# Where the first weight sum of a seven-product matrix multiply is begun: at the fetch of its first block, or at the cast of that block

## The chip, the cores and the metric

The kernel runs on one core of a Trainium2 chip. The metric is device time in microseconds (us) of one execution. Engines are named as in the profile: PE is TensorE (matrix multiplies), ACT is ScalarE, DVE is VectorE, POOL is GpSimd, SP is SyncE. SP issues plain loads; POOL issues the transfers that add into their destination.

## The reference

The program is a small encoder: two layers, 528 tokens (512 and 16 learned ones), width 1024. Each layer has a feed-forward half, a mixer (gated linear attention beside softmax attention) and a second feed-forward half:

```python
def swiglu(x, w_gate, w_up, w_down):
    return (jax.nn.silu(x @ w_gate) * (x @ w_up)) @ w_down
...
for l in range(DEPTH):
    h = h + 0.5 * swiglu(rmsnorm(h, norm_gains[l, 0]), ...)
    h = h + mixer(rmsnorm(h, norm_gains[l, 1]), ...)
    h = h + 0.5 * swiglu(rmsnorm(h, norm_gains[l, 2]), ...)
```

The change concerns the four feed-forward blocks alone. Their hidden width is 2816. In the names of tiles and in this document they are blocks 00, 01, 10 and 11 (layer, then first or second half), in this order of time.

## The kernel before

**Seven products.** A gate and an up column block of 256 hidden channels make one *pair*; there are eleven, numbered 0 to 10. A pair's weights are cut into four blocks called 11, 12, 21 and 22, each a tile of 128 x 1024 float32 (512 KB). Instead of eight products of quarter blocks the kernel makes seven, in the manner of Winograd. Three use a weight block as it was loaded: product 1 uses 11, product 2 uses 12, product 4 uses 22. Four use sums of blocks:

- product 7 uses s3 = 21 - 11,
- product 6 uses s2 = 22 + s3,
- product 5 uses s1 = 21 + 22,
- product 3 uses s4 = s2 - 12.

The first eight pairs' down projections are made the same way; their weights are the entries 11 to 14 (two for each of the first two groups of four pairs). So a feed-forward block has 15 entries in the order 0, 1, 2, 3, 11, 12, 4, 5, 6, 7, 13, 14, 8, 9, 10.

**How a sum is made.** s3 starts as a negation of block 11 on ACT (`negative`, line 203), and POOL then issues a transfer that adds block 21 from DRAM to it (`add`, line 208). s2 starts as a load of block 22 on SP, and POOL adds s3 to it from SBUF. s1 starts as a load of 21, and POOL adds 22 from DRAM. s4 is, from entry 2 on, a subtraction on DVE (line 233); for the entries 0 and 1 it is a negation and an addition as s3 is. In the trace s3 and s4 are the tiles `s`, and s2 and s1 are tiles `w`, so the three additions read `s<-win`, `w<-s` and `w<-win`. s3 and s4 share three buffers (`wsa`), s2 and s1 three others (`wsb`), and loaded blocks three (`wraw`).

**Cast and use.** `make` splits each operand for PE: ACT rounds it to `whi` (line 264), DVE subtracts to get `wlo` (line 265). There are four buffers of each, so a cast can run at most three products ahead of PE: it waits until the product four before it is done. `fetch` runs further ahead, nine loads (`AHEAD_FETCHED`). In steady state the products of two neighbouring pairs alternate in the order 1, 7 (of the pair before), 2, 4 and 3 (of the pair before), 6, 5. Behind products 1, 6 and 7 ACT takes a copy of the PSUM accumulator (line 575, "the copy" below), and the next casts are placed behind that copy. At the end of the first two groups the seven products of the down projection stand between the pairs (line 685, with additions into `h` at line 693 and the casts of their operands at lines 646 and 647). That stretch is called the *group end* below.

**Order.** Each engine works off its instructions strictly in the order in which they stand. That order is not written by hand: a planner goes through the program with priorities in the order of the source and costs of its own, and places an instruction early if it takes its inputs to be ready by then. So an edit in one place can move instructions elsewhere.

Of the kernel before, what the change touches and what calls it, by code (L numbers as in the profile page):

```python
# [14 lines left out]
ALU = mybir.AluOpType  # L15
# [31 lines left out]
OPENING = ((0, 0), 0), ((0, 0), 1)  # L47
# [123 lines left out]
class Weights:  # L171
# [34 lines left out]
    def add(self, t, src):  # L206

        self.nc.gpsimd.dma_start(t, src, accum_op=ALU.add)  # L208

    def sums(self, f, i, product, w):  # L210


        got = self.summed
        if product == "1":
            s3 = self.negative(f, i, "s3", w)
            self.add(s3, self.dram(f, i, "21"))
            s2 = self.block(f, i, "22", self.short, "wsb")
            self.add(s2, s3)
            got[f, i, "7"], got[f, i, "6"] = s3, s2
        if product == "12"[(f, i) in OPENING]:  # L220
            s1 = self.block(f, i, "21", self.short, "wsb")
            self.add(s1, self.dram(f, i, "22"))
            got[f, i, "5"] = s1
        late = 2 <= i
        if product == "2" and not late:
            s4 = self.negative(f, i, "s4", w)
            self.add(s4, got[f, i, "6"])
            got[f, i, "3"] = s4
        if product == "2" and late:
            self.kept = w  # L230
        if product == "6" and late:
            s4 = self.long.tile([P, SLAB], F32, tag="wsa", name=f"s4_{f[0]}{f[1]}_{i}")
            self.nc.vector.tensor_tensor(s4, w, self.kept, ALU.subtract)
            got[f, i, "3"] = s4

    def fetch(self, upto):

        while self.fetched < min(upto, len(self.loads)):
            load = self.loads[self.fetched]
            if isinstance(load, int):  # L240
                w = self.raw.tile([P, SLAB], F32, tag="raw", name=f"raw{load}")
                self.nc.sync.dma_start(w, self.wts[load])
                self.raws[self.fetched] = w
            elif load[2] in DIRECT:
                self.raws[self.fetched] = self.block(*load[:2], DIRECT[load[2]])
                if load[2] == "1" and load[:2] not in OPENING:
                    self.sums(*load, self.raws[self.fetched])
            self.fetched += 1

    def make(self, upto):  # L250
        nc = self.nc
        while self.made < min(upto, len(self.loads)):
            self.fetch(self.made + 1)
            s = self.made
            load = self.loads[s]
            w = self.raws.pop(s, None)
            if w is None:
                w = self.summed.pop(load)
            hi = self.hi_pool.tile([P, SLAB], F32R, tag="whi", name=f"whi{s}")
            lo = self.lo_pool.tile([P, SLAB], F32R, tag="wlo", name=f"wlo{s}")  # L260
            for a in np.split(np.arange(SLAB), 2 if s == 0 else 1):
                cs = slice(a[0], a[-1] + 1)
                with self.tc.issue_after(self.behind) if self.behind else nullcontext():
                    nc.scalar.copy(hi[:, cs], w[:, cs])  # L264
                nc.vector.tensor_tensor(lo[:, cs], w[:, cs], hi[:, cs].bitcast(F32), ALU.subtract)  # L265
            self.got[s] = (hi, lo)
            self.got.pop(s - 12, None)
            self.made += 1
            if not isinstance(load, int) and (load[2] in "26" or load[2] == "1" and load[:2] in OPENING):
                self.sums(*load, w)  # L270

    def use(self, j, ahead=AHEAD_MADE):
# [29 lines left out]
def build(tc, ctx, xt, wts, win, par, w2, const, umask, out):  # L302
# [243 lines left out]
    def ffn(l, f, norm, done, following):  # L546

        x, rs, up, n = norm.x, None, None, live[0]
        w = n // 2
        pools = open_pools("left", psum=("s2",), c=4, s2=2)  # L550
        made, hid, sums, raw, sets = {}, {}, {}, {}, {}
        risen = iter(range(KC))

# [636 lines left out]
    def finish_chunk(c):  # L1190
        fin.square(c)
        gain(c, slice(0, SEQ))

    def ending(sums, operand, rs):

        table("abs_reciprocal_sqrt_and_small")
# [146 lines left out]
```

## Time and profile before

| | |
|---|---|
| time before, median of 3 runs | 2238.69 us (2238.67 to 2239.18) |
| profiled execution: its own time | 2233.24 us |
| profiled execution: its span, first to last instruction | 2231.4 us |
| granted TensorE clock, mean | 0.996 |
| PE busy | 2170.3 us, 97% |
| DVE busy | 1700.7 us, 76% |
| ACT busy | 1244.2 us, 56% |
| POOL busy | 164.4 us, 7% |

The page gives each engine's busy time. The list of waits says which engine sat idle before which instruction, and what ended the wait. The timeline lists instructions of an engine in order of time, with the idle time before each in brackets and its releaser. A table by windows gives busy time, the granted clock of TensorE ("PEclk", 1.00 is full speed) and the share of time in which the 16 DMA engines worked.

### The profile page before, as it was taken

How to read it: one execution, taken by the hardware profiler on the slowest of the kernel's cores; microseconds unless marked ns; L12 is line 12 of the kernel's file. 1: busy time of each engine (PE TensorE's matmuls, PEld its weight loads, DVE VectorE, ACT ScalarE, POOL GpSimd, SP SyncE). 2: the span in 40 equal slices, each digit the busy share in tenths (PEclk: the TensorE clock that was granted, in tenths of full speed). 3: DMA queues.
4: the chain of work that ended last, by engine and by line, in shares of the span. 5: the costliest groups of instructions: out<-in, count | busy, mean ns of one | idle time of the engine just before them, and what ended most of it. 6: DMA issues, size and time to landing. Idle time of an engine off the chain costs nothing. (4 is left out here: it accounts for less than half of the span.)

```text
span 2231.4 us, 40120 instructions
## 1 busy us (share of the span) xinstructions
PE 2170.3 (97%) x16506; PEld 2075.3 (93%) x16506; DVE 1700.7 (76%) x2623; ACT 1244.2 (56%) x1815; POOL 164.4 (7%) x192
## 2 busy tenths in 40 slices
PE   7999999999999999999999999999999999999898
PEld 7999999989999999999999999999788888999897
DVE  8877877577876679687788778676779768687777
ACT  8555555345784555454675455553557836545553
POOL 1111100000000011111011111000000001111100
PEclk9999999999999999999999999999999999999999
DMA  9877753212114577777668777421111237677761
GB/s 280 226 190 203 198 150 109 77 48 72 43 39 133 133 189 191 211 203 190 179 166 212 190 208 202 139 100 67 57 67 57 88 104 199 177 200 191 187 180 67
DMA packets 92647, 330.29 MB, mean 148 GB/s; under 512 B 10288, under 2 KB 12720, under 8 KB 92464
## 3 DMA queue, kind: packets, MB, share of 16 engines
q1 hardware_dynamic: 63440, 226.65, 28.2%
q0 software_dynamic: 27072, 98.58, 24.4%
q8 instruction: 130, 2.13, 0.4%
q10 hardware_dynamic: 1952, 2.50, 0.4%
q14 instruction: 53, 0.43, 0.1%
HBM read 289.94 MB, written 2.10 MB: 131 GB/s over the span
## 5 line engine op out<-in xcount | busy, mean ns | idle before, releaser
L571 PE MATMUL ss<-xc,whi 128*128 128x264 f32 (+1 forms) x4928 | 909.2, 286 | 26.1 <-ACT c L575 16.5
L571 PEld LDWEIGHTS ss<-xc,whi 128*128 128x128 f32 x4928 | 768.8, 190 | 31.1 <-ACT c L575 18.8
L571 PE MATMUL ss<-xc,wlo 128*128 128x264 f32 (+1 forms) x2464 | 702.8, 285 | 2.7 <-DVE wlo L265 2.7
L265 DVE TENSOR_TENSOR wlo<-w,whi 128x1024 fp32r<-128x1024 f32 (+1 forms) x301 | 365.3, 1216 | 152.8 <-ACT whi L264 152.7
L571 PEld LDWEIGHTS ss<-xc,wlo 128*128 128x128 f32 x2464 | 467.4, 190 | 4.3 <-DVE wlo L265 4.3
L264 ACT CAST whi<-w 128x1024 fp32r<-128x1024 f32 (+1 forms) x301 | 312.1, 1048 | 136.2 <-PE ss L571 52.2
L438 PE MATMUL mm<-x,whi 128*128 128x264 f32 (+1 forms) x1712 | 384.8, 315 | 0.0
L438 PEld LDWEIGHTS mm<-x,whi 128*128 128x128 f32 x1712 | 278.4, 188 | 16.6 <-issue 1.0
L438 PE MATMUL mm<-x,wlo 128*128 128x264 f32 (+1 forms) x856 | 266.1, 315 | 0.0
L685 PE MATMUL ss<-g,whi 128*128 128x264 f32 (+1 forms) x1280 | 239.5, 285 | 4.4 <-DVE h L693 3.1
L264 ACT CAST whi<-raw 128x1024 fp32r<-128x1024 f32 x126 | 132.0, 1048 | 163.6 <-PE mm L438 102.8
L685 PEld LDWEIGHTS ss<-g,whi 128*128 128x128 f32 x1280 | 198.6, 188 | 7.0 <-ACT whi L264 3.4
L265 DVE TENSOR_TENSOR wlo<-raw,whi 128x1024 fp32r<-128x1024 f32 x126 | 153.9, 1221 | 59.3 <-ACT whi L264 58.4
L685 PE MATMUL ss<-g,wlo 128*128 128x264 f32 (+1 forms) x640 | 181.2, 283 | 0.0
L575 ACT COPY c<-ss 128x528 f32<-128x528 f32 (+1 forms) x132 | 78.3, 593 | 181.6 <-PE ss L571 181.4
L265 DVE TENSOR_TENSOR wlo<-s,whi 128x1024 fp32r<-128x1024 f32 x120 | 146.5, 1221 | 37.5 <-ACT whi L264 37.5
L438 PEld LDWEIGHTS mm<-x,wlo 128*128 128x128 f32 x856 | 159.6, 188 | 8.5 <-issue 0.7
L438 PE MATMUL ss<-g,whi 128*128 128x264 f32 (+2 forms) x900 | 166.2, 299 | 0.0
L438 PEld LDWEIGHTS ss<-g,whi 128*128 128x128 f32 x900 | 131.7, 188 | 5.3
L264 ACT CAST whi<-s 128x1024 fp32r<-128x1024 f32 x120 | 126.1, 1051 | 10.9 <-PE ss L571 7.2
L208 POOL DMA_DIRECT2D w<-win x60 | 54.5, 908 | 1029.3 <-DVE wlo L265 410.3
L203 ACT ACTIVATE s<-w 128x1024 f32<-128x1024 f32 x68 | 71.6, 1056 | 89.7 <-DMA w<-win 77.9
(265 smaller groups left out, 3405.4 us busy)
## 6 DMA issues: line engine op xcount, KB each, us to landing
w<-win SPq DMA_DIRECT2D x299, 512.0 KB, 5.4
raw<-wts SPq DMA_DIRECT2D x126, 512.0 KB, 3.2
s<-win POOLq DMA_DIRECT2D x60, 512.0 KB, 5.2
w<-s POOLq DMA_DIRECT2D x60, 512.0 KB, 5.5
w<-win POOLq DMA_DIRECT2D x60, 512.0 KB, 7.5
s<-w POOLq DMA_DIRECT2D x8, 512.0 KB, 8.4
h<-xt SPq DMA_DIRECT2D x3, 528.0 KB, 6.3
out<-h ACTq DMA_DIRECT2D x4, 256.0 KB, 2.4
```

Source lines behind the costliest of these rows:

```text
L203: self.nc.scalar.activation(t, w, AF.Copy, scale=-1.0)
L208: self.nc.gpsimd.dma_start(t, src, accum_op=ALU.add)
L264: nc.scalar.copy(hi[:, cs], w[:, cs])
L265: nc.vector.tensor_tensor(lo[:, cs], w[:, cs], hi[:, cs].bitcast(F32), ALU.subtract)
L438: TE.matmul(acc.half[i][:width], lhs, rhs[:, acc.spans[i]], start=first, stop=last)
L571: TE.matmul(acc[:, j], a[:, j, k], b[:, at], start=bool(begin and k == 0 and i == 0), stop=k == len(x) - 1 and i == 2, skip_group_check=no ...
L575: W.behind = S.copy(part(st, q), acc).ins
L685: TE.matmul(acc[:, j], a[:, j, k], xs[b][:, k], start=bool(begin and k == 0 and i == 0), stop=k == 3 and i == 2, skip_group_check=not begin)
```

## The change

For entries from 2 on, the negation for s3 and the two additions behind it (21 into s3, s3 into s2) are no longer written where block 11 is fetched, but where block 11 has been cast (`sums` called from `make` with product 1). What stays at the fetch is the load of 22 for s2, and the load and addition for s1. Entries 0 and 1 keep their place. No instruction is added or removed, and none works on other data.

```diff
-    def sums(self, f, i, product, w):
+    def begin_sums(self, f, i, w=None):
         got = self.summed
-        if product == "1":
+        s3 = None
+        if i < 2:
             s3 = self.negative(f, i, "s3", w)
             self.add(s3, self.dram(f, i, "21"))
-            s2 = self.block(f, i, "22", self.short, "wsb")
+        s2 = self.block(f, i, "22", self.short, "wsb")
+        if i < 2:
             self.add(s2, s3)
-            got[f, i, "7"], got[f, i, "6"] = s3, s2
-        if product == "12"[(f, i) in OPENING]:
-            s1 = self.block(f, i, "21", self.short, "wsb")
-            self.add(s1, self.dram(f, i, "22"))
-            got[f, i, "5"] = s1
...
+        got[f, i, "7"], got[f, i, "6"] = s3, s2
+        if (f, i) not in OPENING:
+            self.first_sum(f, i)
+
+    def first_sum(self, f, i):
+        s1 = self.block(f, i, "21", self.short, "wsb")
+        self.add(s1, self.dram(f, i, "22"))
+        self.summed[f, i, "5"] = s1
+
+    def sums(self, f, i, product, w):
...
+        elif product == "1":
+            got[f, i, "7"] = self.negative(f, i, "s3", w)
+            self.add(got[f, i, "7"], self.dram(f, i, "21"))
+            self.add(got[f, i, "6"], got[f, i, "7"])
...
                 if load[2] == "1" and load[:2] not in OPENING:
-                    self.sums(*load, self.raws[self.fetched])
+                    self.begin_sums(*load[:2], self.raws[self.fetched])
...
-            if not isinstance(load, int) and (load[2] in "26" or load[2] == "1" and load[:2] in OPENING):
+            if not isinstance(load, int) and load[2] in "126":
                 self.sums(*load, w)
```

More of the change, by code (lines that the diff above doesn't have):

```diff
@@ L208, in add @@
         self.nc.gpsimd.dma_start(t, src, accum_op=ALU.add)
-    def sums(self, f, i, product, w):
+    def begin_sums(self, f, i, w=None):
         got = self.summed
-        if product == "1":
+        s3 = None
+        if i < 2:
             s3 = self.negative(f, i, "s3", w)
             self.add(s3, self.dram(f, i, "21"))
-            s2 = self.block(f, i, "22", self.short, "wsb")
+        s2 = self.block(f, i, "22", self.short, "wsb")
+        if i < 2:
             self.add(s2, s3)
-            got[f, i, "7"], got[f, i, "6"] = s3, s2
-        if product == "12"[(f, i) in OPENING]:
-            s1 = self.block(f, i, "21", self.short, "wsb")
-            self.add(s1, self.dram(f, i, "22"))
-            got[f, i, "5"] = s1
[L224 to L229, printed above, removed]
+        got[f, i, "7"], got[f, i, "6"] = s3, s2
[6 more added lines that the diff above has]
+    def sums(self, f, i, product, w):
+        got, V = self.summed, self.nc.vector
+        if (f, i) in OPENING and product in "12":
+            (self.begin_sums if product == "1" else self.first_sum)(f, i, *[w] * (product == "1"))
+        if i < 2:
+            if product == "2":
+                s4 = self.negative(f, i, "s4", w)
+                self.add(s4, got[f, i, "6"])
+                got[f, i, "3"] = s4
+        elif product == "1":
+            got[f, i, "7"] = self.negative(f, i, "s3", w)
+            self.add(got[f, i, "7"], self.dram(f, i, "21"))
+            self.add(got[f, i, "6"], got[f, i, "7"])
+        elif product == "2":
             self.kept = w
-        if product == "6" and late:
+        elif product == "6":
             s4 = self.long.tile([P, SLAB], F32, tag="wsa", name=f"s4_{f[0]}{f[1]}_{i}")
-            self.nc.vector.tensor_tensor(s4, w, self.kept, ALU.subtract)
+            V.tensor_tensor(s4, w, self.kept, ALU.subtract)
             got[f, i, "3"] = s4
```

## The prediction

> **What bounds the kernel now.** I read the page first, then the list of waits, then the timelines of ACT, PE, DVE and POOL around PE's longest waits, then windows for the granted clock and the DMA engines.
>
> ```profile
> span 2231.4 us, 40120 instructions
> PE 2170.3 (97%) x16506; PEld 2075.3 (93%) x16506; DVE 1700.7 (76%) x2623; ACT 1244.2 (56%) x1815; POOL 164.4 (7%) x192
> ACT s L203 <- DMA w<-win: 77.9, 18, 6.3
> PE ss L571 <- ACT c L575: 16.5, 11, 4.8
> PE ss L685 <- DVE h L693: 3.1, 2, 1.6
> ```
>
> PE is the bound. The negation (`ACT s L203`) waits 77.9 us for its block to land, but ACT has room; such a wait costs only what PE loses by it. PE loses in few places: 16.5 us to copies of its accumulator, in 11 waits. The two longest have one cause. The first, on ACT:
>
> ```profile
> 1935.81 0.83 ACT L646 CAST g<-g 128x768 fp32r<-128x768 f32 x1
> 1942.97 1.06 ACT L203 ACTIVATE s<-w 128x1024 f32<-128x1024 f32 x1 [6.33 <-DMA w<-win]
> 1944.66 0.58 ACT L575 COPY c<-ss 128x512 f32<-128x512 f32 x1
> 1944.43 0.88 POOL L208 DMA_DIRECT2D s<-win  x1 [9.49 <-ACT s L203]
> ```
>
> The negation of entry 12 in block 11 waits 6.33 us for its block; the copy that PE needs stands behind it. POOL issues the first addition 0.4 us after the negation's end (1942.97 + 1.06 to 1944.43). On PE, with the same place of entry 14 and one of block 00:
>
> ```profile
> 1945.29 0.50 PE L571 MATMUL ss<-xc,whi 128*128 128x256 f32 x2 [4.84 <-ACT c L575]
> 2076.43 0.58 PE L571 MATMUL ss<-xc,whi 128*128 128x256 f32 x1 [4.79 <-ACT c L575]
> 98.07 0.51 PE L571 MATMUL ss<-xc,whi 128*128 128x264 f32 x2 [0.50 <-ACT c L575]
> ```
>
> A long wait costs twice, for the clock falls behind it:
>
> ```profile
> 1945.50:1949.00 3.50, 3.50 (x19) 3.50 (x19) 3.44 (x5) 1.62 (x2) 0.00 (x0) 0.53 0.81 150
> 1962.00:1966.00 4.00, 1.31 (x8) 0.74 (x6) 3.76 (x6) 3.61 (x4) 0.00 (x0) 1.00 0.67 200
> 1966.00:1970.00 4.00, 4.00 (x21) 4.00 (x22) 3.93 (x4) 0.00 (x0) 0.00 (x0) 0.57 0.02 4
> 2076.40:2082.00 5.60, 5.57 (x26) 5.58 (x27) 3.73 (x6) 2.08 (x3) 0.91 (x2) 0.50 0.54 97
> ```
>
> (Columns: window, length, busy time of PE, PE loads, DVE, ACT, POOL, then granted clock, DMA share, GB/s.)
>
> **What the change moves.** In the order that the planner gives the changed program, four things differ; no instruction is added. (1) The negation of most entries stands one to four casts later on ACT. (2) Its two additions go to POOL's queue as much later, and for the entries 3, 5, 6, 7, 9, 10, 11 and 13 of nearly every block the addition into s1 now stands ahead of that into s2. (3) In block 11 PE's order at the group ends, the odd one of four before, becomes that of the other three blocks. (4) DVE's subtraction for s4, which reads the finished s2, stands *earlier* in most entries, by one to four casts: the planner holds s2 for ready there. SP changes places of neighbouring loads only; what it waits for (free buffers) is as before, so I cost that at nothing, or part of the fourth rival if it is not.
>
> **The gain: block 11.** Entry 12's negation now stands two casts and one copy later, entry 14's too, where the blocks have landed. The waits 4.84 and 4.79 fall to the 0.50 that block 00 shows, and the two waits for `h` at L693 (3.1 together) belong to the odd order: 4.34 + 4.29 + 3.1 = 11.7 us. The low clock goes too: 3.5 x 0.47 + 4.0 x 0.43 + 5.6 x 0.50 = 6.2 us. Sum 17.9; I take 17, since shorter waits stay at the same places. What is late next there is the copy itself, at 0.50.
>
> **The first loss: entry 2 in block 00.** The subtraction for s4 now stands ahead of four updates of `h`, of the products into `g` and of the `wlo` of product 2.
>
> ```profile
> 61.91 0.60 ACT L575 COPY c<-ss 128x528 f32<-128x528 f32 x1 [1.33 <-PE ss L571]
> 63.16 1.06 ACT L264 CAST whi<-w 128x1024 fp32r<-128x1024 f32 x1 [0.64 <-DMA w<-s]
> 56.05 2.56 DVE L732 SCALAR_TENSOR_TENSOR h<-h,rs 128x528 f32<-128x528 f32 x4
> 58.52 0.76 DVE L625 TENSOR_TENSOR g<-c 128x264 f32<-128x264 f32 x2
> 59.83 1.21 DVE L265 TENSOR_TENSOR wlo<-w,whi 128x1024 fp32r<-128x1024 f32 x1
> 63.23 1.23 DVE L233 TENSOR_TENSOR s<-w,w 128x1024 f32<-128x1024 f32 x1
> w<-s POOLq DMA_DIRECT2D x1, 512.0 KB, 9.7
> ```
>
> The cast at 63.16 was released by the addition into s2 (9.7 us from issue to landing, the last row, of the window 53.4 to 54.3), so DVE stands from about 56 to 63.1. Then come the subtraction (1.23), two updates (2 x 0.64), the `g` pair (0.76) and `wlo` (1.21): 67.6. PE begins product 2 when the copy at 61.91 begins, and its third multiply, some 0.2 us on, needs `wlo`: it stands for 5.5 us. The negation moves one cast (1.05 us) here, against one addition less in the queue beside it (that of entry 3); I take nothing for both, bounds -1 and +1. A wait of that length cools the clock as the two above did: one stretch of 3.5 us gives 1.7, two give 2.8 as in the row of 5.6 us; I take 1.7. Together 7.2 (4.5 to 9.3).
>
> **The second loss: entry 2 in block 10.** The subtraction now stands ahead of three of five updates and of the `wlo` of product 4.
>
> ```profile
> 1170.62 2.01 ACT L264 CAST whi<-w 128x1024 fp32r<-128x1024 f32 x2
> 1174.33 1.05 ACT L264 CAST whi<-w 128x1024 fp32r<-128x1024 f32 x1 [1.71 <-PE ss L571]
> 1164.38 3.18 DVE L732 SCALAR_TENSOR_TENSOR h<-h,rs 128x528 f32<-128x528 f32 x5
> 1169.16 1.23 DVE L265 TENSOR_TENSOR wlo<-w,whi 128x1024 fp32r<-128x1024 f32 x1 [1.60 <-ACT whi L264]
> ```
>
> s2 is there when its cast starts, 1170.62. Then 1.23 + 3 x 0.64 + 1.23 give 1175.0. The cast at 1174.33 was released by the end of that product, which takes 2.93 us (below), so PE began it at 1171.4 and now stands from 1171.6 to 1175.0: 3.4 us. Does the clock fall? PE was idle for 2.7 of the 4 us before 1966, and 0.57 followed; 3.4 us spread over two of its spells may or may not do that. I take half of 1.7: 4.2 (3.0 to 5.1).
>
> The Trainium skill ("TensorE: Matmul & The Clock Gate", Part 1) lets the clock fall only after a whole idle window of about 3.4 us. By that the wait would just miss it, and the loss would be 3.4; the row of 1.31 us busy in 4 shows that less idling is enough, and I go by the row.
>
> **The third loss: entries 5 and 9 of every block.** The cast of the s1 of entry 4 frees the way for entry 5's negation, which now stands behind it; behind it, DVE's subtraction stands ahead of the `wlo` of product 2 and of an addition into `h` that frees the accumulator for that product.
>
> ```profile
> 129.75 1.05 ACT L264 CAST whi<-w 128x1024 fp32r<-128x1024 f32 x1 [0.94 <-ACT g L646]
> 144.34 1.05 ACT L264 CAST whi<-w 128x1024 fp32r<-128x1024 f32 x1 [0.90 <-PE ss L571]
> 167.77 1.05 ACT L264 CAST whi<-w 128x1024 fp32r<-128x1024 f32 x1 [0.31 <-PE ss L571]
> 157.16 1.22 DVE L265 TENSOR_TENSOR wlo<-w,whi 128x1024 fp32r<-128x1024 f32 x1 [1.16 <-ACT whi L264]
> 159.10 0.70 DVE L693 TENSOR_TENSOR h<-h,ss 128x528 f32<-128x528 f32 x1 [0.72 <-PE ss L685]
> 154.00:158.00 4.00, 4.00 (x35) 4.00 (x34) 2.84 (x4) 1.25 (x2) 0.00 (x0) 1.00 1.05 235
> w<-s POOLq DMA_DIRECT2D x1, 512.0 KB, 8.0
> s<-win POOLq DMA_DIRECT2D x60, 512.0 KB, 5.2
> w<-s POOLq DMA_DIRECT2D x60, 512.0 KB, 5.5
> w<-win POOLq DMA_DIRECT2D x60, 512.0 KB, 7.5
> ```
>
> The casts at 144.34 and 167.77 were released by the ends of two products eight apart: 23.43 / 8 = 2.93 us each. The later is product 2 of entry 5, so PE begins it at 164.8. The chain: entry 4's negation stands behind the cast at 129.75, done at 131.9; issue 0.4, landing 5.2: 137.5; its other two additions go out 0.4 and 1.3 later, the second lands 7.5 on, at 146.3, 2 us after the old 144.34. Then cast and negation (2.1) 148.4, issue 0.4, landing 5.2, issue 0.4: 154.4. The addition into s2 takes between the median 5.5 and the 8.0 of this very entry (the row with x1): 159.9 to 162.4. Now it stands behind that into s1, and the DMA engines are full here (share 1.05), so I also allow 2 more: 164.4. Subtraction, `wlo` and `h` add 1.23 + 1.22 + 0.70: 163.1 to 167.6, against 164.8. PE's loss lies between nothing and 2.8; I take 1.2, near the middle, for the full engines speak against the lower end. In block 11 the products are shorter (256 columns, not 264, 0.1 us each, seven of them), so 1.9 there. Six times 1.2 and twice 1.9: 11 (0 to 24).
>
> **The rest.** Entries 3, 6, 7 and 10 have the same chain, with one or two more products between; I take 2 for a few short waits (0 to 5). The later additions of entries 4 and 8 still land some 3 us before PE, being cast three products ahead; nothing, or part of the fourth rival.
>
> Sum: -17 + 7.2 + 4.2 + 11 + 2 = +7.4. The profiled execution took 2233.24 us itself (span 2231.4), 5.4 below the median of 2238.69; I add to the median: 2246 (profiled: 2241). A measurement of this kernel tells 0.2%, 4.5 us, from no change.
>
> **Rivals.** First, the side of faster: the additions are quick enough, as their medians (5.5) say, and entries 5 and 9 fit: -17 + 7.2 + 4.2 + 1 = -5, 2234. It decides at the landing of s2: at 161.6 or before in entry 5. For it speak the medians, against it the DMA share. Chance 0.22, half of it beyond 0.2%. Second, faster still: the early subtractions hurt nowhere and only the gain is left, 2222. That needs s2 of entry 2 to land before 59 in block 00, where the row shows 63.16; 0.08. Third, slower: the gain does not come, because something else holds the copy in block 11, while the losses do: 2263; 0.07. Fourth, slower: the additions lag by a further 2.5 us in entries 5 and 9, with the full DMA engines, from the point where s2 lands after 164: 8 x 2.5 = 20 more, 2266; 0.17. My forecast has 0.46, its own range 2239 to 2256.
>
> **The numbers.** Faster: 0.08 and half of 0.22, 0.19. Same: the other 0.11 and the low edge of my own case, 0.12: 0.23. Slower: 0.58. The range leaves out the second rival and the upper half of the third and fourth: 2230 to 2263.
>
> **What would show it.** After: no wait over 1 us of PE for a copy at the group ends of block 11, and no clock under 1 there; DVE idle before the s4 subtraction of entry 2 in block 00 from 56 to about 63 and PE idle some 5 us at 62 on an L265 `wlo`; 3 us of the same in block 10; short waits of PE, eight times, on `h` at the product behind the group ends. It is wrong if PE's new waits on DVE sum to under 12 us or over 40, or if block 11 keeps its waits.

## The result: 73 us slower, most of it at entries 5 and 9, at six times the price forecast for them

| | before | after |
|---|---|---|
| median, runs of one chip | 2238.93 us (2238.67 to 2241.81, 4 runs) | 2312.39 us (2310.57 to 2316.54, 4 runs) |
| ratio, 95% interval | | 1.0328 [1.031, 1.0346] |
| span of the profiled execution | 2231.4 us | 2309.8 us |
| PE busy | 2170.3 us | 2194.2 us |

The forecast was 2246 (2230 to 2263). In the new kernel lines behind the diff stand 15 higher: L586 is the pair products' multiply, L590 the copy, L708 the addition into `h`, L279 and L280 the casts; L248 is the subtraction for s4.

From the page of after:

```profile
span 2309.8 us, 40158 instructions
PE 2194.2 (95%) x16506; PEld 2093.3 (91%) x16506; DVE 1702.9 (74%) x2623; ACT 1246.6 (54%) x1815; POOL 164.6 (7%) x192
L248 DVE TENSOR_TENSOR s<-w,w 128x1024 f32<-128x1024 f32 x52 | 63.6, 1222 | 165.8 <-DMA w<-s 93.3
s<-win POOLq DMA_DIRECT2D x60, 512.0 KB, 7.7
```

From its list of waits (engine, what it was to do, releaser: total us, times, longest):

```profile
PE ss L586 <- DVE h L708: 45.0, 8, 6.8
PE ss L586 <- DVE wlo L280: 18.7, 16, 5.2
PE ss L586 <- ACT c L590: 7.0, 10, 1.6
PE ss L700 <- ACT g L661: 4.5, 5, 1.4
```

PE's waits for copies fell from 16.5 to 7.0 us: the gain of block 11 came. In its place stand eight waits for `h`, 45.0 us together, and 18.7 us for `wlo` (2.7 before). DVE waits 165.8 us in front of its subtraction for s4, where it waited 0.1 us before; the addition of 21 into s3 takes 7.7 us to land, where before it took 5.2. The group of the subtraction in the kernel before:

```profile
L233 DVE TENSOR_TENSOR s<-w,w 128x1024 f32<-128x1024 f32 x52 | 63.4, 1219 | 0.1
```

The first of the eight, entry 5 of block 00, in the timelines of DVE, POOL and PE:

```profile
176.48 1.23 DVE L248 TENSOR_TENSOR s<-w,w 128x1024 f32<-128x1024 f32 x1 [10.76 <-issue]
177.62 1.22 DVE L280 TENSOR_TENSOR wlo<-w,whi 128x1024 fp32r<-128x1024 f32 x1
178.76 0.70 DVE L708 TENSOR_TENSOR h<-h,ss 128x528 f32<-128x528 f32 x1
168.79 0.86 POOL L208 DMA_DIRECT2D w<-s  x1 [5.99 <-issue]
179.60 0.78 PE L586 MATMUL ss<-xc,whi 128*128 128x264 f32 x2 [5.77 <-DVE h L708]
```

The same stretch in windows (columns as in the prediction), and the transfer issued at 168.79:

```profile
174.00:179.50 5.50, 0.00 (x0) 0.00 (x0) 3.02 (x4) 2.46 (x3) 0.00 (x0) 0.94 0.12 24
179.50:183.00 3.50, 3.40 (x15) 3.43 (x16) 3.46 (x5) 0.00 (x0) 0.00 (x0) 0.50 0.80 204
183.00:187.00 4.00, 4.00 (x25) 4.00 (x24) 2.53 (x3) 1.96 (x2) 0.00 (x0) 0.66 0.61 217
```

```profile
w<-s POOLq DMA_DIRECT2D x1, 512.0 KB, 7.6
```

The addition into s2 went out at 168.79 and took 7.6 us: s2 was there at 176.4. DVE's subtraction waited for it ("issue" is the page's word where it sees no releaser; the landing, 0.1 us before, is the one that fits), with the `wlo` of product 2 and the addition into `h` queued behind it; PE started when that addition was done. The idle stretch then cooled the clock to 0.50 and 0.66, which costs 3.5 x 0.50 + 4 x 0.34 = 3.1 us more. By PE's starts of the same products in both traces, the eight places cost 6.9 to 9.8 us each, 64.6 together.

**Why s2 was so late.** Entry 4's addition into s3 in the timelines of POOL, DVE and SP, and then the transfers issued in the 5.5 us from there on. First of before:

```profile
124.61 0.86 POOL L208 DMA_DIRECT2D s<-win  x1 [12.07 <-ACT s L203]
131.15 1.22 DVE L233 TENSOR_TENSOR s<-w,w 128x1024 f32<-128x1024 f32 x1
132.44 3.78 SPq L198 DMA_DIRECT2D w<-win  x4
```

```profile
s<-win POOLq DMA_DIRECT2D x1, 512.0 KB, 5.2
w<-win SPq DMA_DIRECT2D x1, 512.0 KB, 4.2
```

Then of after, where the answer for the transfers covers the group's four loads:

```profile
139.58 0.86 POOL L208 DMA_DIRECT2D s<-win  x1 [20.18 <-ACT s L203]
138.57 1.22 DVE L248 TENSOR_TENSOR s<-w,w 128x1024 f32<-128x1024 f32 x1
139.86 0.81 SPq L198 DMA_DIRECT2D w<-win  x2
```

```profile
w<-win SPq DMA_DIRECT2D x4, 512.0 KB, 7.2
s<-win POOLq DMA_DIRECT2D x1, 512.0 KB, 7.8
```

In both kernels a group of four plain loads begins to leave SP as soon as the subtraction for s4 of the entry before has released its buffer (131.15 + 1.22 and 132.44; 138.57 + 1.22 and 139.86). Before, the addition into s3 was 8 us ahead of that group and had landed. Now it goes out 0.3 us ahead of it, and takes 7.8 us. Entry 5's used to go out 3.6 us ahead of its own group (142.91 and 146.52); now it goes out 2.6 us behind the first load of it (160.55 and 157.99). Counted over the landing time of that addition in block 00, the mean number of plain loads in flight rose from 0.31 to 2.70 for entry 4 (5.2 to 7.8 us) and from 0.59 to 2.19 for entry 5 (5.1 to 7.6).

### The profile page after: what moved, and what is told of

Same layout as the page of the kernel before. It is cut to its first block, busy times and chain, and to the rows that moved or that the text cites. A ratio compares the mean times of both kernels' runs of the same rounds, so it can differ in the third digit from the quotient of the medians.

```text
span 2309.8 us, 40158 instructions
## 1 busy us (share of the span) xinstructions
PE 2194.2 (95%) x16506; PEld 2093.3 (91%) x16506; DVE 1702.9 (74%) x2623; ACT 1246.6 (54%) x1815; POOL 164.6 (7%) x192
## 5 line engine op out<-in xcount | busy, mean ns | idle before, releaser
L586 PE MATMUL ss<-xc,whi 128*128 128x264 f32 (+1 forms) x4928 | 926.3, 289 | 64.0 <-DVE h L708 45.0
L586 PEld LDWEIGHTS ss<-xc,whi 128*128 128x128 f32 x4928 | 782.0, 193 | 71.5 <-issue 46.9
L586 PE MATMUL ss<-xc,wlo 128*128 128x264 f32 (+1 forms) x2464 | 711.4, 289 | 18.9 <-DVE wlo L280 18.7
L586 PEld LDWEIGHTS ss<-xc,wlo 128*128 128x128 f32 x2464 | 475.1, 193 | 23.1 <-DVE wlo L280 22.9
L279 ACT CAST whi<-w 128x1024 fp32r<-128x1024 f32 (+1 forms) x301 | 312.8, 1047 | 233.0 <-PE ss L586 95.5
L280 DVE TENSOR_TENSOR wlo<-w,whi 128x1024 fp32r<-128x1024 f32 (+1 forms) x301 | 365.3, 1216 | 70.7 <-ACT whi L279 70.6
L700 PE MATMUL ss<-g,whi 128*128 128x264 f32 (+1 forms) x1280 | 239.8, 285 | 5.0 <-ACT g L661 4.5
L279 ACT CAST whi<-raw 128x1024 fp32r<-128x1024 f32 x126 | 132.1, 1048 | 163.9 <-PE mm L453 102.8
L700 PEld LDWEIGHTS ss<-g,whi 128*128 128x128 f32 x1280 | 198.5, 188 | 7.8 <-ACT g L661 5.5
L280 DVE TENSOR_TENSOR wlo<-raw,whi 128x1024 fp32r<-128x1024 f32 x126 | 153.9, 1221 | 57.9 <-ACT whi L279 56.9
L590 ACT COPY c<-ss 128x528 f32<-128x528 f32 (+1 forms) x132 | 78.4, 594 | 211.1 <-PE ss L586 211.0
L248 DVE TENSOR_TENSOR s<-w,w 128x1024 f32<-128x1024 f32 x52 | 63.6, 1222 | 165.8 <-DMA w<-s 93.3
L700 PE MATMUL ss<-g,wlo 128*128 128x264 f32 (+1 forms) x640 | 181.3, 283 | 0.0
L280 DVE TENSOR_TENSOR wlo<-s,whi 128x1024 fp32r<-128x1024 f32 x120 | 146.4, 1220 | 39.3 <-ACT whi L279 39.3
L279 ACT CAST whi<-s 128x1024 fp32r<-128x1024 f32 x120 | 125.9, 1049 | 3.0 <-PE ss L586 2.2
```

Of the source, the lines that this page charges most:

```text
L248: V.tensor_tensor(s4, w, self.kept, ALU.subtract)
L586: TE.matmul(acc[:, j], a[:, j, k], b[:, at], start=bool(begin and k == 0 and i == 0), stop=k == len(x) - 1 and i == 2, skip_group_check=no ...
L590: W.behind = S.copy(part(st, q), acc).ins
L700: TE.matmul(acc[:, j], a[:, j, k], xs[b][:, k], start=bool(begin and k == 0 and i == 0), stop=k == 3 and i == 2, skip_group_check=not begin)
```

## The experiments

Each was compared with the kernel before on the same chip (medians of before 2239.6 to 2240.3). "Held back" below means this edit, with the entries named:

```diff
-                nc.vector.tensor_tensor(lo[:, cs], w[:, cs], hi[:, cs].bitcast(F32), ALU.subtract)
+                self.lo_ins = nc.vector.tensor_tensor(lo[:, cs], w[:, cs], hi[:, cs].bitcast(F32), ALU.subtract).ins
...
-            V.tensor_tensor(s4, w, self.kept, ALU.subtract)
+            with self.tc.issue_after(self.lo_ins) if i in (5, 9) else nullcontext():
+                V.tensor_tensor(s4, w, self.kept, ALU.subtract)
```

**1. DVE's order: s4 of entries 5 and 9 held back.** PE's order stays as in the changed kernel. One thing moves besides: in eight places, behind the stretch in question, the next entry's two additions into s1 and s2 change places on POOL.

> The changed kernel, with DVE's subtraction for s4 of entries 5 and 9 held behind the wlo of product 6 of the same entry; chain of additions as in the changed kernel. Theory 1 (head of the line: PE waits because the wlo of product 2 and the addition into h stand behind a subtraction that waits for s2, not because PE's own operands are late): the eight waits of 4.6 to 6.8 us for h go, with the low clock behind them, together 64 us by PE's starts (8 places of 6.9 to 9.5); time 2248, and PE has no wait over 1.2 us at product 6 of these entries, whose wlo is then ready some 3 us ahead. Theory 2 (the operands themselves are late; DVE's order only says where it shows): PE waits as long two or three products later, for the wlo of product 6 or 5 of the same entries; time 2290 or more.

Measured 2249.32 us, ratio 1.0042 [1.0025, 1.0059]. From its timeline of DVE and its list of waits:

```profile
172.10 1.23 DVE L281 TENSOR_TENSOR wlo<-w,whi 128x1024 fp32r<-128x1024 f32 x1 [4.92 <-ACT whi L280]
177.91 1.22 DVE L249 TENSOR_TENSOR s<-w,w 128x1024 f32<-128x1024 f32 x1
```

```profile
PE ss L587 <- DVE wlo L281: 18.4, 19, 4.1
```

s2 of entry 5 landed as late as without the edit (175.0 in this trace, 5.6 us behind the start of the copy before it; 5.5 in the changed kernel), the `wlo` of product 2 ran without it, and none of the eight waits for `h` is left. Theory 1 holds: what costs 63 us is who stands behind the subtraction, not the operands' own lateness.

**2. POOL's order alone: the addition into s2 ahead of that into s1.**

```diff
-        self.add(s1, self.dram(f, i, "22"))
+        if i < 2:
+            self.add(s1, self.dram(f, i, "22"))
...
-            self.add(got[f, i, "6"], got[f, i, "7"])
+            second = self.add(got[f, i, "6"], got[f, i, "7"])
+            with self.tc.issue_after(second):
+                self.add(got[f, i, "5"], self.dram(f, i, "22"))
```

> The changed kernel, with the addition into s1 placed behind that into s2 on POOL for every entry from 2 on; no other engine's order differs. Theory 1a (s2 is late because the addition into s1 runs beside the first two): in entries 5 and 9 s21 minus 11 lands in 5.2 us instead of 7.6 and s2 in 5.5 instead of 7.6, s2 comes 4.5 us earlier, PE's eight waits fall from 5.6 to about 1 and most of the low clock goes: 8 x 6.6 = 53 us, time 2260. Theory 1b (the transfers are slow whatever stands beside them on that queue, since the DMA engines are full with loads): s2 comes less than 1.5 us earlier, time 2300 or more.

Measured 2299.76 us, ratio 1.0272 [1.0255, 1.0289]. From its list of waits, and from its page:

```profile
PE ss L589 <- DVE h L711: 29.6, 8, 5.1
```

```profile
s<-win POOLq DMA_DIRECT2D x60, 512.0 KB, 7.5
w<-s POOLq DMA_DIRECT2D x60, 512.0 KB, 5.2
```

The waits for `h` fell from 45.0 to 29.6 us. The addition into s2 took a microsecond less in the median (5.2, and 6.2 in the changed kernel); that into s3 did not (7.5). So neither 1a nor 1b whole: the neighbour on the queue costs the second step, not the first, and about a third of the waits.

**3. Entries 4 and 8 begun at the fetch.** In `begin_sums` and `sums` the test on `i` becomes `i in MOVED`, a list of entries; here all from 2 on but 4 and 8.

> The changed kernel, with entries 4 and 8 begun at the fetch as before; only ACT's order differs (their negations). Theory 1c (entry 5 is late because its negation stands behind the cast of the s1 of entry 4, itself late): that cast comes about 4.2 us earlier, so does s2 of entries 5 and 9, PE's waits fall from 5.6 to 1.4, the 1.1 us at entries 4 and 8 go too, and most of the low clock: 8 x 7.3 = 58 us, time 2254. If entry 4 is not what delays entry 5, the waits stay over 4 us and only 8 x 1.1 = 9 us go: 2303.

Measured 2248.92 us, ratio 1.0044 [1.0029, 1.0059]. DVE's order is that of the changed kernel, and the subtraction still waits, but less (timeline of DVE, then the list of waits):

```profile
169.15 1.23 DVE L249 TENSOR_TENSOR s<-w,w 128x1024 f32<-128x1024 f32 x1 [7.00 <-issue]
```

```profile
PE ss L587 <- DVE h L709: 7.6, 8, 1.8
```

Theory 1c holds: 45.0 became 7.6 us, and behind the first of the eight, now 1.2 us long, the granted clock is 1.00 where it was 0.50. Entry 5's own additions into s3 and s2 still took 7.4 and 7.6 us there; what went is their late start. Experiments 1 and 3 take away one factor each, and each wins some 63 us (some 10 of them, in 3, at entries 4 and 8 themselves): the loss needs the early place on DVE *and* the late entry before it.

**4. The transfers by themselves.** A kernel of rounds: a negation on ACT releases one addition on POOL and n loads on SP, the first load some 0.3 us ahead of the addition.

> No encoder here: everything is left out but rounds of transfers of 512 KB, and the output is zeros. In each round ACT's negation releases one addition on POOL (from DRAM) and n plain loads on SP, n = 0, 1, 2, 3, 4 in turn, 8 rounds each; then 8 rounds each of an addition from SBUF with 0 and with 3 loads beside, and 8 of an addition with a second addition behind it. If the addition is slowed by loads that go out with it: 5.1 us from issue to landing with none, about 6 with one, 7.7 with three, 8.5 or more with four; one from SBUF 4.7 alone and over 6.5 beside three; a second addition costs the first 1 us or more. If its time doesn't depend on what goes out with it, all stay within 5.0 to 5.6.

The transfers issued in a stretch of eight rounds: the addition from DRAM with no load, with one (and that load), with four; then that from SBUF (`s<-s`) with none and with three:

```profile
s<-win POOLq DMA_DIRECT2D x8, 512.0 KB, 5.4
s<-win POOLq DMA_DIRECT2D x8, 512.0 KB, 7.7
raw<-win SPq DMA_DIRECT2D x8, 512.0 KB, 3.8
s<-win POOLq DMA_DIRECT2D x8, 512.0 KB, 8.9
s<-s POOLq DMA_DIRECT2D x8, 512.0 KB, 4.5
s<-s POOLq DMA_DIRECT2D x8, 512.0 KB, 9.5
```

The first theory holds, and steeper than expected: one load is enough for 7.7; with two the median is 8.0, with three 8.7. With a second addition behind it the first stayed at 5.1 to 5.5 us and the second took 6.9 to 7.3, which is experiment 2 in small. What was shown here is the mechanism in isolation; no run took the loads away alone in the encoder. The traces of the encoder agree in part. Sorted by the mean number of loads in flight (under 0.7, to 1.5, to 2.5, above), the 60 additions into s3 of the changed kernel took 6.4, 7.3, 7.8 and 8.3 us in the median (9, 19, 20 and 12 of them). In the kernel before, the first three classes took 5.1, 5.3 and 6.1 us (36, 10 and 13). So the time rises with the loads in both, but at an equal count the changed kernel is slower still, and the cause of that remainder is open.

**5. One part at a time: entries 4 and 8, entries 5 and 9, entry 2.**

> The change for entries 4 and 8 alone; against the kernel before only ACT's order differs, in eight places. If the addition of 21 goes out together with the loads that the same cast releases: it lands in 7.7 us instead of 5.2, the casts of s2 and s1 of these entries come some 6 and 5 us later, PE stands about 1.1 us there, eight times, and nowhere for h: 2240 + 9 = 2249. If the lateness of entries 4 and 8 alone carries over to 5 and 9: waits of over 2 us there and 2265 or more. By the recorded forecast nothing: 2240.

> The change for entries 5 and 9 alone, with DVE's subtraction early there as in the changed kernel. If it takes the late entry before it for the long waits: s2 lands some 4 us earlier against PE than in the changed kernel, PE waits 1 to 2 us for h, eight times, without a low clock: 2240 + 8 x 1.2 = 2250. If moving 5 and 9 is enough for the long waits: 8 x 8 = 64 more, 2300.

> The change for entry 2 alone. PE's starts in the changed kernel put its cost at 7.2 us in block 00 and 6.05 in block 10, nothing in the others: 2240 + 13 = 2253. If these losses were paid back elsewhere or came from later entries: 2245 or less.

Measured 2270.00 us (1.0129 [1.0114, 1.0144]), 2240.14 (1.0003 [0.9994, 1.0013]) and 2238.89 (0.9994 [0.9984, 1.0003]). None of the three came out by its reasoning; 2270 and 2238.89 lie where a second branch put the time (2265 or more, 2245 or less), but for other causes.

For the latter two the premise was wrong: with so little moved, the planner put the subtraction back to where it stood before, behind the `wlo` of product 6 (entries 5 and 9; entry 2 likewise stayed behind product 2's), and then the late additions cost nothing that can be measured. That is experiment 1 once more, from the other side. Entries 4 and 8 alone cost 30 us where 9 were expected. PE's waits for `wlo` rose from 2.7 to 10.2 us, about as expected; but those for copies rose from 16.5 to 30.0, which I had not foreseen. On ACT and PE of that kernel:

```profile
169.60 1.06 ACT L204 ACTIVATE s<-w 128x1024 f32<-128x1024 f32 x1 [9.77 <-DMA w<-win]
171.99 0.60 ACT L591 COPY c<-ss 128x528 f32<-128x528 f32 x1
172.64 0.59 PE L587 MATMUL ss<-xc,whi 128*128 128x264 f32 x1 [2.93 <-ACT c L591]
```

Entry 6's negation, still written at the fetch, waits 9.77 us for its block, and the copies that PE needs stand behind it: the wait that block 11 had in the kernel before, now in other blocks. The changed kernel, in which entry 6's negation moves too, has 7.0 us of waits for copies in all.

**6. Entry 2 held back as well, and then 4 and 8 begun at the fetch.** As in 1, with `i in (2, 5, 9)`; the second also with the list of 3.

> The changed kernel, with DVE's subtraction for s4 of entries 2, 5 and 9 held behind the wlo of product 6 of the same entry. If the waits of entry 2 in blocks 00 and 10 come from DVE's order as those of 5 and 9 do: the 7.2 and 6.05 us that PE's starts gave for them in the changed kernel go on top of what the kernel with 5 and 9 alone won: 2249.3 - 13.2 = 2236, and no wait of PE over 2 us is left there. If late additions alone hold PE there: 2247 or more.

> As the kernel before in this list (subtraction for entries 2, 5 and 9 held back), and entries 4 and 8 begun at the fetch. If the ledger adds up, the 8 x 1.1 us at entries 4 and 8 go too, and what is left of the change is the gain of block 11 and of the group ends: 2236 - 9 = 2227. If the chains of the other entries still cost something with DVE's order mended, 2234 or more.

Measured 2241.05 us (1.0007 [0.9997, 1.0017]), not the 2236 expected, and 2227.54 (0.9942 [0.9927, 0.9957]). The waits of entry 2 went in both blocks, but in block 00 the next subtraction took its place (DVE, then PE, first kernel):

```profile
84.91 1.23 DVE L249 TENSOR_TENSOR s<-w,w 128x1024 f32<-128x1024 f32 x1 [8.29 <-DMA w<-s]
87.32 0.59 PE L587 MATMUL ss<-xc,wlo 128*128 128x264 f32 x1 [3.42 <-DVE wlo L281]
```

This is entry 3's, 8.29 us idle on DVE; so 8 us were won by the medians and not 13. The second kernel came out at the 2227 expected, but 13.5 us below the first, where the eight small waits of entries 4 and 8 explain 9 or 10; so that hit is in part luck.

**7. Entries 11 to 14 alone** (the list of 3, with these four).

> The change for entries 11 to 14 alone; 2 to 10 begin their sums at the fetch as before. If gain and losses of the change are apart in place, the gain of block 11 is left: PE's starts put it at 15.6 us (8.3 and 7.3), time 2223. If the gain hangs on entries 3 and 7 being moved too, or the places of 11 and 13 bring waits of their own, time 2235 to 2240.

Measured 2212.23 us, ratio 0.9876 [0.9861, 0.9891]: faster than both. From its list of waits; then block 11's first group end in the timelines of ACT and PE; then a window of it:

```profile
PE ss L587 <- ACT c L591: 8.6, 12, 1.6
```

```profile
1934.45 0.59 ACT L591 COPY c<-ss 128x512 f32<-128x512 f32 x1 [1.30 <-PE ss L587]
1936.84 1.05 ACT L204 ACTIVATE s<-w 128x1024 f32<-128x1024 f32 x1
1935.09 0.50 PE L587 MATMUL ss<-xc,whi 128*128 128x256 f32 x2 [0.50 <-ACT c L591]
```

```profile
1957.00:1963.00 6.00, 6.00 (x54) 6.00 (x53) 6.00 (x7) 4.41 (x5) 0.89 (x1) 1.00 0.22 23
```

The negation of entry 12 now stands behind the copy and waits for nothing, no wait of PE for the group ends' additions into `h` is left, and the clock stays at 1.00. Its span is 22.1 us under that of before: by PE's starts 18.1 come from block 11 and the rest from the group ends of the other blocks. The medians differ by 28; the profiled execution of before was itself 5.4 under its median, this one 1.1. The 2223 expected was 11 us too high: block 11 gave more than 15.6, the other blocks were left out, and the rest is that difference between execution and median.

## Why the prediction was right about the places and wrong about the price

By PE's starts of the same products in the two profiled executions (their spans differ by 78.4 us, the medians by 73.5):

| step of the prediction | forecast | measured |
|---|---|---|
| gain, block 11 | -17 | -15.6 (-18.1 alone) |
| entry 2, block 00 | +7.2 | +7.4 |
| entry 2, block 10 | +4.2 | +6.05 |
| entries 5 and 9 | +11 | +64.6 |
| entries 4 and 8 | nothing | +10.2, eight times 0.4 to 1.8 |
| the rest | +2 | +5.7 |

**The gain** came as argued, waits and clock. The negation's place and PE's order changed there together, and no run separates them.

**Entry 2.** In block 00 the chain was right; the wait came a little shorter (5.18, not 5.5) and the clock cost a little more (2.2, not 1.7), so the sum is closer than its terms. The third row is block 10's (after, timelines of DVE and PE):

```profile
63.65 1.23 DVE L248 TENSOR_TENSOR s<-w,w 128x1024 f32<-128x1024 f32 x1 [6.83 <-DMA w<-s]
67.99 0.59 PE L586 MATMUL ss<-xc,wlo 128*128 128x264 f32 x1 [5.18 <-DVE wlo L280]
1222.80 0.39 PE L586 MATMUL ss<-xc,wlo 128*128 128x264 f32 x1 [4.26 <-DVE wlo L280]
```

In block 10 the wait was 4.26 and not 3.4, and the clock did fall behind it. The rule of the Trainium skill that was weighed there ("TensorE: Matmul & The Clock Gate", Part 1) would have given 3.4 for the forecast wait; 4.26 is longer than its window of about 3.4, so this place does not tell it from the row that I went by. Other runs side with the row: in the kernel with entries 4 and 8 alone a wait of 2.06 us, PE being busy for 0.95 of those 3 us, was followed by a clock of 0.57. But length alone does not decide: in experiment 2 waits of 2.84 and 3.23 us left the clock at 1.00.

**Entries 5 and 9: the step that failed.** The place, the order on DVE and the victim (`wlo` of product 2, then `h`) were right; the landing of s2 was not. From the end of entry 4's negation to the landing of s2 of entry 5 the forecast had at most 32.5 us (131.9 to 164.4); it took 37.2 (139.2 to 176.4). The terms that were too small or missing are both additions of 21 into s3, 7.8 and 7.6 us where I took the median 5.2 of before, and entry 5's negation, which stood 1.6 us for a buffer. The addition into s2 took 7.6 where the forecast allowed 10.0. That is 2.6 + 2.4 + 1.6 - 2.4 = 4.2 of the 4.7 us. The negation (after, timeline of ACT):

```profile
159.08 1.06 ACT L203 ACTIVATE s<-w 128x1024 f32<-128x1024 f32 x1 [1.62 <-DVE wlo L280]
```

The 2 us that I allowed because "the DMA engines are full here" were put on one transfer of the four in this chain, and the one that did not need it. The deeper mistake is the sentence on SP, "what it waits for (free buffers) is as before, so I cost that at nothing, or part of the fourth rival if it is not": SP's loads did stay where they were, and the additions moved into them. A duration from the trace of before belongs to its neighbours there. Then the clock: the wait of 1.2 us in experiment 3 left it alone, that of 5.77 here did not, and I had priced none for this loss. 45.0 us of waits became 64.6 us of loss, mostly by that.

**Entries 4 and 8** were said to land 3 us early. They had 5 us to lose (the addition into s2 used to land 134.92 for a cast at 140.0); the late start and the slower addition took them all, and ACT now waits for the landing, 6.30 us at 153.86, then PE 0.75 for its `wlo`.

**The rest** is not traced further; PE's waits for `g` from ACT at L700 are part of it (0.7 us before, 4.5 now).

**Rivals.** The fourth, additions that lag further with full DMA engines, came nearest to what happened. Over the landing of the additions into s3 of entries 4 and 5 of block 00 the DMA share rose from 0.69 and 0.75 to 0.85 and 0.99. In the rounds a high share as such slowed nothing: over its landing it was 0.71 to 0.74 with a second addition behind, where the first kept its 5.4 us, and 0.63 to 0.65 beside one load, where it took 7.6 to 8.1. Whether that holds in the encoder, no run shows. The rival's lag of 2.5 us was 4.4 (5.6 against the forecast's 1.2), and without the clock it stopped at 2266. The bound of 40 us for PE's new waits on DVE, above which the forecast was to count as wrong, was passed by the waits for `h` alone.

## What to carry to other kernels

When a transfer is moved in time, price it by what it will fly beside, not by its median of before; list what each queue issues within its landing time at the new place. An early place for an instruction that waits on a transfer is a bet by the scheduler: look at who is queued behind it, and at how much that transfer's chain has been stretched elsewhere. And a change that helps in one place and hurts in others is worth cutting down to the place: entries 11 to 14 alone gave 28 us where the whole change lost 73.

## What was not expected of the hardware

An accumulating transfer of 512 KB from DRAM lands in 5.4 us alone, in 7.7 beside a single plain load of the same size, which itself takes 3.8, and in 8.9 beside four; from SBUF, 4.5 alone and 9.5 beside three. A second accumulating transfer behind it on its own queue left the first at 5.1 to 5.5 us. So in these rounds the first load on another engine's queue cost an accumulation from DRAM 2.3 us, three more loads only 1.2 together, and what followed on its own queue nothing.

The Trainium skill ("DMA: Bandwidth & Descriptors", Queues, rings and completion order) says that each DMA engine takes turns between the queues for which it has work, a packet at a time. By that, loads on SP count as one competitor however many there are, and a later transfer on POOL's queue as none. The rounds agree in the second (5.1 to 5.5 with a second addition behind) and nearly in the first (7.7 with one load, 8.9 with four). From SBUF there is no round with one load, so the 5.0 us that three cost there do not test it.
